# Value product of the dilation-16 attention group: rounded weights and their rests in columns of their own

## The chip, the cores and the metric

The program runs on one core of one Trainium2 chip. The metric is the device time of one execution in microseconds (us); lower is better. A core has a matmul engine (TensorE; PE in the profile, PEld for its weight loads), a vector engine (VectorE, DVE), a scalar engine (ScalarE, ACT), GpSimd (POOL) and SyncE (SP), which issues the transfers. Each engine works through its own queue in order.

## The reference, cut to what matters

The reference is one step of a two-layer decoder trunk. Layer 0 mixes tokens with windowed attention in three head groups, with dilations 1, 4 and 16, over 1024 prompt positions and 16 heads of 64 channels; layer 1 pools. A gated two-matrix channel mixer follows each. What the change touches is the attention of the prompt:

```python
s = jnp.einsum("nbqhd,nbkhd->nbhqk", qb, kb).astype(jnp.float32) * SCALE
s = s + bias[:, np.clip(rel, 0, SPAN)]
s = jnp.where(valid[None, :, None], s, NEG_INF)
m = jnp.max(s, axis=-1)
p = jnp.exp(s - m[..., None])
l = jnp.sum(p, axis=-1)
o = jnp.einsum("nbhqk,nbkhd->nbqhd", p.astype(v.dtype), vb).astype(jnp.float32)
...
o = o / l[..., None]
```

The last product, `p` times `vb`, is the value product. All is float32.

## The kernel before, in words

**Split numbers.** The matmuls run on a rounded float32 type. To keep precision each operand is split into a rounded part ("hi") and its rest ("lo"): ACT copies to the rounded type, and another engine subtracts. A projection is then three matmuls for every pair of operands (L120), with weights split into `w_hi` (ACT, L99) and `w_lo` (POOL, L100).

**Units.** The attention is done in 24 units, a unit being a pair of heads `hp` (0 to 7) and a group `g` (2, then 1, then 0). While the projections of one unit run on PE, the attention of the unit before runs between them. After each projection step (three matmuls at L120) the function `between()` advances a clock by one and emits what is due on a list: for block `i` of 128 queries the scores at 6i+1, the transpose of the weights (`probs_t`) at 6i+15, the value product (`pv`) at 6i+24, and for every second block the finish (`finish_o`) at 6i+26. The splitting of the next unit's queries (`pack_q`, L397 to L399) and keys (`pack_k`, L408 to L410) is emitted at clocks 29 to 46.5 and 50 to 59. So each engine's queue has the order of that list.

**One block.** PE makes scores (L455 where a block has 128 keys, L462 where 256). DVE adds the bias (L456) and reduces (L464), ACT takes the exponential (L467). PE transposes the weights into one PSUM buffer `pt` (L475), ACT rounds them into `phl` (L479), DVE subtracts for the rest (L480). The values were transposed earlier, and stand in `vhl`, rounded part and rest side by side (L443, L444).

**The value product.** For each head, `pv_mm` multiplies the 128 columns of `vhl` (64 rounded, 64 rests) first with the rounded weights, then with their rests, accumulating into the same columns of `u.o` (L489). Each block of group 2 takes four matmuls of 128 columns. Half of the partitions of `u.o` then hold the product with the rounded values, the other half the product with the rests of the values. One tile `u.o` (one PSUM bank, three buffers) serves two blocks and both heads. At the end of the second block ACT copies the half with the rests over to the partitions of the other half (L508), and two clocks later `finish_o` adds both halves and puts the sum in place (DVE, L525).

In this document "step 0" to "step 7" are the eight value products of a unit, and "pair 0" to "pair 3" the four pairs of steps that share a finish.

Of the kernel before, what the change touches and what calls it, by code (L numbers as in the profile page):

```python
# [11 lines left out]
F32 = mybir.dt.float32  # L12
F32R = mybir.dt.float32r
AF = mybir.ActivationFunctionType
# [33 lines left out]
def trunk(ctx: ExitStack, tc: tile.TileContext, a, out):  # L48
    nc = tc.nc
# [31 lines left out]
    raws, split, nxt, more = {}, {}, [0, 0, 0], [None]  # L81
# [200 lines left out]
    with ExitStack() as ph:  # L282
        qp = ph.enter_context(tc.tile_pool(name="qkv", bufs=1))
        mmp = ph.enter_context(tc.tile_pool(name="mmp", bufs=1, space=PSUM))
        app = ph.enter_context(tc.tile_pool(name="app", bufs=1, space=PSUM))
# [150 lines left out]
        def transpose_v(u, half):  # L436
            ps = app.tile([128, 4, 2, 64], F32, name="vt", tag="misc")
            for j in range(4):
                i = 4 * half + j
                nc.tensor.transpose(ps[:, j].rearrange("p a d -> p (a d)"),  # L440
                                    u.raw[2][:, T - 128 * i - 128:T - 128 * i], ident)
            v = qp.tile([128, 4, 2, 128], F32R, name="vhl", tag="vhl", bufs=2)
            nc.scalar.activation(v[:, :, :, 0:64], ps, AF.Copy)  # L443
            nc.vector.tensor_sub(v[:, :, :, 64:128], ps, v[:, :, :, 0:64].bitcast(F32))  # L444
            u.v[half] = v

        def scores(u, i):
            w = 256 if has_prev(u.g, i) else 128
# [34 lines left out]
        def pv_mm(u, j, b0, b1, first):  # L483


            q = (j + b0) % 2
            for h in range(2):
                for x in range(2):
                    nc.tensor.matmul(u.o[:, h, 128 * q:128 * (q + b1 - b0)], u.v[j // 4][:, j % 4, h, :],  # L489
                                     u.pt[j][0][:, h, x, 128 * b0:128 * b1], start=first and h + x == 0, stop=True,  # L490
                                     skip_group_check=True)

        def pv(u, j):
            first = j % 2 == 0
            if first:
                u.o = app.tile([128, 2, 256], F32, name="o", tag="o", bufs=3)
                if j and u.pt[j - 1][1] == 256:
                    pv_mm(u, j - 1, 1, 2, True)
                    first = False
            pv_mm(u, j, 0, 1 if j % 2 else u.pt[j][1] // 128, first)  # L500
            if j % 2:

                x = 256 * (j // 2 % 2)
                tmp = (part[:, 0, x:x + 256] if (u.hp, u.g) != order[23] else
                       qp.tile([128, 256], F32, name="ot", tag="ot", bufs=1))
                u.tmp = tmp, u.o
                for h, (own, other) in enumerate(((A, B), (B, A))):
                    nc.scalar.activation(tmp[own], u.o[other, h], AF.Copy)  # L508

        def finish_o(u, i):  # L510

            if i == 0:
                u.og = ogs[0]()[:, :T]
                ogs.rotate(-1)
            tmp, o = u.tmp
            if u.g == 0:
                dst, split = u.og[:, 256 * i:256 * i + 256], lambda t: t
            elif u.g == 1:
                dst = u.og.rearrange("p (n q r) -> p r n q", n=2, r=4)[:, i]
                split = lambda t: t.rearrange("p (n q) -> p n q", n=2)  # L520
            else:
                dst = u.og.rearrange("p (s r) -> p r s", r=16)[:, 4 * i:4 * i + 4]
                split = lambda t: t.rearrange("p (n q) -> p n q", n=4)
            for h, own in enumerate((A, B)):
                nc.vector.tensor_add(dst[own], split(o[own, h]), split(tmp[own]))  # L525


        stat_d = {}
# [278 lines left out]
        def attend(u, tasks, gap=6):  # L807


            u.v, u.p, u.pt = [None, None], {}, {}  # L810
            if u.g:
                u.st = qp.tile([128, 8, 2, 2], F32, name="st", tag=f"st{u.g}", bufs=2)
            else:
                u.others = qp.tile([128, 3, 8, 2, 2], F32, name="st", tag="st0", bufs=2)
                u.st = u.others[:, 0]
            steps = []
            for i in range(8):
                steps += [(6 * i + 1, lambda i=i: scores(u, i)), (6 * i + 15, lambda i=i: probs_t(u, i)),
                          (6 * i + 24, lambda i=i: pv(u, i))]
                if i % 2:  # L820
                    steps.append((6 * i + 24 + 2, lambda i=i: finish_o(u, i // 2)))
            for half in range(2):
                steps.append((24 * half + 4, lambda half=half: transpose_v(u, half)))

            def others():
                for g in range(2):
                    nc.sync.dma_start(out=u.others[:, 1 + g].rearrange("p b h e -> p b (h e)"),
                                      in_=stat_d[u.hp][g].rearrange("(b p) e -> p b e", p=128))

            if u.g == 0:  # L830
                steps.append((26, others))
            steps.append((47, lambda: store_stats(u)))
            for i in range(tasks):
                steps += [(gap * i + 4, lambda: task(extra)), (gap * i + 7, lambda: task(behind))]
            plan.extend(sorted(steps, key=lambda x: x[0]))
            clock[0] = 0.0
# [64 lines left out]
        for n, (hp, g) in enumerate(order):  # L901
            u = units[hp, g] = Unit()
# [8 lines left out]
            for i, (which, c) in enumerate(seq):  # L911
# [12 lines left out]
                ps = mmp.tile([128, 352], F32, name="mm", tag="mm", bufs=2)  # L924
# [58 lines left out]
        for n, ct in enumerate(OUT):  # L983
# [9 lines left out]
            for c in range(3):  # L993
                c0, c1 = CHUNKS[c]
                ps = mmp.tile([128, 352], F32, name="mm", tag="mm", bufs=2)
# [416 lines left out]
```

## Time and profile before

| | |
|---|---|
| median of 3 runs | 2903.01 us (2902.28 to 2905.36) |
| the profiled execution | 2902.76 us, span 2900.8 us |
| PE busy | 2786.3 us (96%) |
| DVE, ACT, POOL busy | 1629.2 us (56%), 1357.9 us (47%), 1409.8 us (49%) |
| the 24 attention units | about 75 to 1231 us of the span |
| value matmuls (L489) | 864, of which 256 in the 8 units of group 2 |

A view of the profile lists instructions with start (us from the start of the span), duration, engine, line, operation and tiles written and read; `xN` merges N of them. Square brackets hold the time for which the engine was idle before, and what ended the wait. A busy share is an average over the program: what bounds a unit is read from that unit's rows.

### The profile page before, as it was taken

What the parts mean: (1) busy time and instruction counts of PE and PEld (TensorE: products, weight loads), DVE (VectorE), ACT (ScalarE), POOL (GpSimd) and SP (SyncE); (2) the same over time, 40 slices, a digit from 0 to 9 for tenths busy, and PEclk for the clock granted to TensorE, in tenths of its full rate; (3) what the DMA queues carried; (4) which work ended last, traced back from release to release, by engine and by line L of the source; (5) the groups of instructions that cost most, each with busy time, mean ns of one, the idle gap of its engine ahead of it and who ended that gap; (6) DMA issues with size and microseconds to landing.
All of it is one profiled execution on the core that took longest, in us unless ns stands there. A gap on an engine that the chain in (4) does not pass through costs nothing.

```text
span 2900.8 us, 46721 instructions
## 1 busy us (share of the span) xinstructions
PE 2786.3 (96%) x18109; PEld 2741.8 (95%) x18109; DVE 1629.2 (56%) x3196; ACT 1357.9 (47%) x2748; POOL 1409.8 (49%) x999
## 2 busy tenths in 40 slices
PE   6999999999999999999999999988899999999998
PEld 5999999999999999889999999988899999999998
DVE  6666756675666566765323334787756333435555
ACT  5565665566556655534222323445442333334443
POOL 4235443545354435445434434566753443445785
PEclk9999999999999999999999999999999999999999
DMA  3234333433343324438222222333332226223543
GB/s 117 58 85 124 95 86 87 122 90 91 82 128 94 87 86 145 139 95 106 67 73 73 66 73 73 109 103 108 119 103 66 73 67 81 67 72 98 182 139 102
DMA packets 203949, 277.80 MB, mean 96 GB/s; under 512 B 70272, under 2 KB 154096, under 8 KB 203728
## 3 DMA queue, kind: packets, MB, share of 16 engines
q1 hardware_dynamic: 203680, 274.80, 34.3%
q8 instruction: 142, 2.33, 0.3%
q14 instruction: 79, 0.65, 0.1%
q10 hardware_dynamic: 48, 0.02, 0.0%
HBM read 251.89 MB, written 23.34 MB: 95 GB/s over the span
## 4 chain that ended last, share of the span: by engine, by line
PE 77%; DVE 13%; ACT 3%; issue 3%; POOL 2%; DMA 1%; SPq 0%; DVEq 0%; ACTq 0%; POOLq 0%
PE mm L120 68%; PE o L489 2%; DVE k L408 2%; PE s L462 1%; POOL w_lo L100 1%; PE pt L475 1%; DVE conv L1117 1%; DVE conv L1114 1%; DVE x L399 1%; ACT w_hi L99 1%; PE s L455 1%; DVE x L397 1%; DVE sums L1225 1%; DVE sc L634 1%; PE spv L768 1%
## 5 line engine op out<-in xcount | busy, mean ns | idle before, releaser
L120 PE MATMUL mm<-hh,w_hi 128*128 128x352 f32 (+2 forms) x4064 | 1343.9, 331 | 13.9 <-ACT w_hi L99 6.9
L120 PE MATMUL mm<-hh,w_lo 128*128 128x352 f32 (+2 forms) x4064 | 1308.8, 322 | 10.4 <-POOL w_lo L100 10.4
L120 PE MATMUL mm<-hl,w_hi 128*128 128x352 f32 (+2 forms) x4064 | 1308.0, 322 | 2.4 <-DVE hl L255 2.4
L100 POOL TENSOR_TENSOR w_lo<-w_raw,w_hi 128x1024 fp32r<-128x1024 f32 x346 | 848.5, 2456 | 672.1 <-ACT w_hi L99 649.3
L120 PEld LDWEIGHTS mm<-hh,w_hi 128*128 128x128 f32 x4064 | 772.7, 190 | 20.7 <-ACT w_hi L99 7.5
L120 PEld LDWEIGHTS mm<-hh,w_lo 128*128 128x128 f32 x4064 | 771.2, 190 | 13.1 <-POOL w_lo L100 13.1
L120 PEld LDWEIGHTS mm<-hl,w_hi 128*128 128x128 f32 x4064 | 773.2, 190 | 4.7 <-DVE hl L255 3.9
L1114 DVE SCALAR_TENSOR_TENSOR conv<-gate,convp,conv 128x336 f32<-128x336 f32 (+1 forms) x176 | 253.6, 1441 | 428.6 <-ACT conv L1112 412.2
L99 ACT ACTIVATE w_hi<-w_raw 128x1024 fp32r<-128x1024 f32 x348 | 363.4, 1050 | 259.9 <-PE mm L120 240.1
L120 PE MATMUL mm<-gh,w_hi 128*128 128x352 f32 (+2 forms) x1056 | 340.8, 323 | 7.6 <-DVE conv L1104 6.3
L120 PE MATMUL mm<-gh,w_lo 128*128 128x352 f32 (+2 forms) x1056 | 340.1, 322 | 3.5 <-POOL w_lo L100 3.5
L120 PE MATMUL mm<-gl,w_hi 128*128 128x352 f32 (+2 forms) x1056 | 339.8, 322 | 0.6 <-POOL gl L1106 0.6
L1052 DVE TENSOR_TENSOR x<-x,mm 128x352 f32<-128x352 f32 (+2 forms) x312 | 157.1, 511 | 257.1 <-PE mm L120 256.5
L467 ACT ACTIVATE p<-p,st 128x128 f32<-128x128 f32 (+1 forms) x384 | 170.0, 443 | 202.4 <-DVE st L464 201.7
L1106 POOL TENSOR_TENSOR gl<-conv,gh 128x352 fp32r<-128x352 f32 (+2 forms) x132 | 124.5, 944 | 238.1 <-ACT gh L1105 233.4
L120 PEld LDWEIGHTS mm<-gh,w_hi 128*128 128x128 f32 x1056 | 199.6, 189 | 9.3 <-DVE conv L1104 7.6
L120 PEld LDWEIGHTS mm<-gh,w_lo 128*128 128x128 f32 x1056 | 200.1, 189 | 4.4 <-POOL w_lo L100 4.4
L120 PEld LDWEIGHTS mm<-gl,w_hi 128*128 128x128 f32 x1056 | 199.8, 189 | 1.1 <-POOL gl L1106 1.1
L480 DVE TENSOR_TENSOR phl<-pt,phl 128x512 fp32r<-128x512 f32 (+1 forms) x192 | 104.6, 545 | 164.2 <-ACT phl L479 163.1
L368 ACT ACTIVATE raw<-mm 128x336 f32<-128x336 f32 (+1 forms) x216 | 144.5, 670 | 102.5 <-PE mm L120 99.1
L1101 ACT ACTIVATE conv<-conv 128x688 f32<-128x688 f32 (+1 forms) x88 | 55.9, 635 | 275.1 <-DVE conv L1114 137.2
L1097 ACT ACTIVATE gate<-mm 128x352 f32<-128x352 f32 (+2 forms) x132 | 59.8, 454 | 224.1 <-PE mm L120 222.5
(190 smaller groups left out, 3190.3 us busy)
## 6 DMA issues: line engine op xcount, KB each, us to landing
w_raw<-in_w_in SPq DMA_DIRECT2D x176, 512.0 KB
w_raw<-in_w_out SPq DMA_DIRECT2D x88, 512.0 KB
w_raw<-in_w_qkv SPq DMA_DIRECT2D x72, 512.0 KB
x<-qd SPq DMA_DIRECT2D x48, 256.0 KB
kc<-in_cache_k SPq DMA_DIRECT2D x48, 256.0 KB
vc<-in_cache_v SPq DMA_DIRECT2D x48, 256.0 KB
x<-c_d SPq DMA_DIRECT2D x42, 256.0 KB
out_new_k<-raw SPq DMA_DIRECT2D x8, 516.0 KB
```

The lines of the kernel that those rows point to most:

```text
L99: nc.scalar.activation(hi, raw, AF.Copy)
L100: (eng or nc.gpsimd).tensor_sub(lo, raw, hi.bitcast(F32))
L120: nc.tensor.matmul(ps, l, r, start=first and i == 0, stop=last and i == n - 1)
L368: nc.scalar.activation(stream(raw[:, :T], u.g, c0, t1, which > 0), ps[:, :w].rearrange("p (s r) -> p s r", r=DILS[u.g]), AF.Copy, scale=si ...
L408: nc.vector.tensor_copy(keys[h][own, 0, t], raw[own, t])
L467: nc.scalar.activation(p[:, h, :w], p[:, h, :w], AF.Exp, bias=u.st[:, i, h, 0:1], scale=-1.0, accum_out=u.st[:, i, h, 1:2])
L480: nc.vector.tensor_sub(phl[:, :, 1, :w], ps[:, :, :w], phl[:, :, 0, :w].bitcast(F32))
L489: nc.tensor.matmul(u.o[:, h, 128 * q:128 * (q + b1 - b0)], u.v[j // 4][:, j % 4, h, :], u.pt[j][0][:, h, x, 128 * b0:128 * b1], start=firs ...
L1052: nc.vector.tensor_add(xT[ct][:, c0:c1], xT[ct][:, c0:c1], ps)
L1097: nc.scalar.activation(gate[:, 2 + s:2 + e], group(tiles8(w, c), c), AF.Copy)
L1106: nc.gpsimd.tensor_sub(self.gl[f][:, s:e], conv[:, s:e], self.gh[f][:, s:e].bitcast(F32))
L1114: nc.vector.scalar_tensor_tensor(conv[:, :n], gate[:, j:j + n], cw[j], conv[:, :n], op0=ALU.mult, op1=ALU.add)
```

## The change

Only group 2 (the one with dilation 16, where each block reads its own 128 keys) takes another value product. The rounded weights and their rests lie side by side as 256 moving columns, and one matmul per head puts their two products into columns of their own. A pair of blocks therefore has two output tiles `u.o`, one for each head, each with 256 columns of the rounded weights and 256 of the rests. The values of the second head are stored rest first, so that in both heads the wanted partitions hold the product with the rounded values. When the second block is done, ACT copies the product of the value rests with the rounded weights as before, and a new DVE addition adds to it the product of the rounded values with the weight rests. The finish adds the last part. The product of value rests with weight rests is not used any more in group 2. The three buffers of `u.o` stay three.

```diff
-            v = qp.tile([128, 4, 2, 128], F32R, name="vhl", tag="vhl", bufs=2)
-            nc.scalar.activation(v[:, :, :, 0:64], ps, AF.Copy)
-            nc.vector.tensor_sub(v[:, :, :, 64:128], ps, v[:, :, :, 0:64].bitcast(F32))
-            u.v[half] = v
+            v = qp.tile([128, 4, 4, 64], F32R, name="vhl", tag="vhl", bufs=2)
+            hi, lo = v[:, :, 0:4:3], v[:, :, 1:3]
+            nc.scalar.activation(hi, ps, AF.Copy)
+            nc.vector.tensor_sub(lo, ps, hi.bitcast(F32))
+            u.v[half] = v.rearrange("p j x d -> p j (x d)").rearrange("p j (h e) -> p j h e", h=2)
...
         def pv_mm(u, j, b0, b1, first):
+            if u.g == 2:
+                for h in range(2):
+                    nc.tensor.matmul(u.o[h][:, :, 128 * (j % 2):128 * (j % 2) + 128], u.v[j // 4][:, j % 4, h, :],
+                                     u.pt[j][0][:, h, :, 0:128], start=first, stop=True, skip_group_check=True)
+                return
...
         def pv(u, j):
-                u.o = app.tile([128, 2, 256], F32, name="o", tag="o", bufs=3)
+                u.o = [app.tile([128, 2, 256], F32, name="o", tag="o", bufs=3) for _ in range(2 if u.g == 2 else 1)]
+                if u.g < 2:
+                    u.o = u.o[0]
...
                 for h, (own, other) in enumerate(((A, B), (B, A))):
-                    nc.scalar.activation(tmp[own], u.o[other, h], AF.Copy)
+                    nc.scalar.activation(tmp[own], u.o[h][other, 0] if u.g == 2 else u.o[other, h], AF.Copy)
+                    if u.g == 2:
+                        nc.vector.tensor_add(tmp[own], u.o[h][own, 1], tmp[own])
...
         def finish_o(u, i):
-                nc.vector.tensor_add(dst[own], split(o[own, h]), split(tmp[own]))
+                nc.vector.tensor_add(dst[own], split(o[h][own, 0] if u.g == 2 else o[own, h]), split(tmp[own]))
```

## Rows read from the trace of the kernel before

**Rows 1.** The page: PE's busy time, and the chain that ended last.
```profile
PE 2786.3 (96%) x18109; PEld 2741.8 (95%) x18109; DVE 1629.2 (56%) x3196; ACT 1357.9 (47%) x2748; POOL 1409.8 (49%) x999
...
PE 77%; DVE 13%; ACT 3%; issue 3%; POOL 2%; DMA 1%; SPq 0%; DVEq 0%; ACTq 0%; POOLq 0%
```

**Rows 2.** Timeline of PE, head pair 2: a value step of group 2.
```profile
397.39 0.56 PE L489 MATMUL o<-phl,vhl 128*128 128x128 f32 x4
...
398.00 0.32 PE L120 MATMUL mm<-hl,w_hi 128*128 128x352 f32 x1
398.16 0.32 PE L120 MATMUL mm<-hh,w_lo 128*128 128x352 f32 x1
```

**Rows 3.** The same, a score block: two matmuls of 256 columns.
```profile
390.98 0.40 PE L455 MATMUL s<-k,x 128*128 128x256 f32 x2
391.22 0.32 PE L120 MATMUL mm<-hh,w_hi 128*128 128x344 f32 x1
```

**Rows 4.** Groups by line and shape: of that unit alone, then of all units.
```profile
L489 PE MATMUL o<-phl,vhl 128*128 128x128 f32 x32 | 4.5, 261 | 0.0
...
L525 DVE TENSOR_TENSOR x<-o,ot 64x256 f32<-64x256 f32 x8 | 3.3, 416 | 0.1
```

**Rows 5.** Timeline of ACT and DVE, head pair 2, pair 0.
```profile
381.28 0.77 ACT L508 ACTIVATE part<-o 64x256 f32<-64x256 f32 x2 [0.25 <-PE o L489]
...
382.06 0.42 DVE L456 TENSOR_TENSOR p<-s,bias 128x256 f32<-128x256 f32 x1 [0.81 <-PE s L455]
...
387.89 0.42 DVE L480 TENSOR_TENSOR phl<-pt,phl 128x256 fp32r<-128x256 f32 x1
```

**Rows 6.** Timeline of ACT and DVE, head pair 2, from pair 1 on.
```profile
390.80 0.77 ACT L508 ACTIVATE part<-o 64x256 f32<-64x256 f32 x2
...
390.81 0.43 DVE L480 TENSOR_TENSOR phl<-pt,phl 128x256 fp32r<-128x256 f32 x1 [1.38 <-ACT phl L479]
391.42 0.42 DVE L456 TENSOR_TENSOR p<-s,bias 128x256 f32<-128x256 f32 x1 [0.18 <-PE s L455]
...
394.58 0.17 DVE L371 TENSOR_SCALAR ks<-mm 128x8 f32<-128x8 f32 x1 [0.25 <-ACT raw L368]
...
401.11 1.23 DVE L525 TENSOR_TENSOR x<-o,part 64x256 f32<-64x256 f32 x2
```

**Rows 7.** Timeline of PE, head pair 2: steps 1 and 6, and a wait.
```profile
380.69 0.56 PE L489 MATMUL o<-phl,vhl 128*128 128x128 f32 x4
...
388.37 0.44 PE L475 MATMUL pt<-consts,p 128*128 128x128 f32 x2 [0.55 <-DVE phl L480]
...
400.86 0.56 PE L489 MATMUL o<-phl,vhl 128*128 128x128 f32 x4
```

**Rows 8.** Timeline of PE, head pair 3: steps 6 and 7.
```profile
542.20 0.56 PE L489 MATMUL o<-phl,vhl 128*128 128x128 f32 x4
545.46 0.22 PE L489 MATMUL o<-phl,vhl 128*128 128x128 f32 x1
547.60 0.55 PE L489 MATMUL o<-phl,vhl 128*128 128x128 f32 x3 [1.92 <-DVE phl L480]
```

**Rows 9.** Chain that ended last in 517 to 552 us (head pair 3).
```profile
531.16 0.44 DVE p L456
...
534.34 0.17 DVE ks L371
...
545.14 0.50 DVE x L525
...
545.65 0.59 DVE x L525
...
547.12 0.43 DVE phl L480
```

**Rows 10.** Stretches: PE, PEld, DVE, ACT, POOL busy, granted clock, DMA, GB/s.
```profile
500.00:501.70 1.70, 0.51 (x4) 0.51 (x5) 1.56 (x7) 0.72 (x2) 0.00 (x0) 1.00 0.00 0
501.70:505.10 3.40, 3.40 (x14) 3.40 (x13) 2.08 (x9) 1.92 (x4) 0.82 (x1) 0.50 0.30 119
```

## The prediction

> **What bounds the kernel now.** The page comes first: PE is busy for 96% of the span and holds 77% of the chain that ended last, DVE 13% [rows 1]. Read over the whole program, that says that fewer matmuls are time saved. But the change sits in eight stretches of some 30 us, the units of group 2, so their rows were read next, engine by engine. In an even unit (head pair 2) PE runs on with one wait for DVE, 0.55 us before the transpose at 388.37 [rows 7]. In an odd unit (head pair 3) DVE sets the pace at the end: the chain of that stretch enters DVE at 531.16, passes through ACT and the projection evacuations without slack to 534.34 and stays on DVE's queue until the weight rests at 547.12 [rows 9], while PE stands 1.92 us in the middle of step 7 [rows 8]. The reason is the same everywhere: the splitting of the next unit's keys and queries is queued on DVE between the value steps. So a matmul saved on PE is worth its time only where DVE is not late, and every DVE instruction added ahead of that backlog is worth its full time.
>
> **The change part by part.**
>
> *Matmuls.* A unit of group 2 has 32 value matmuls of 128 columns [rows 4], four to a step. In step 5 of head pair 2 they begin at 397.39 and the second projection matmul behind them at 398.00; less the 0.16 of one projection matmul (398.00 to 398.16) the four took 0.45 us [rows 2]. Two matmuls of 256 columns whose moving operand lies in two runs, as the new ones' does, take 0.24 us (390.98 to 391.22) [rows 3]. A step saves 0.21 us; 64 steps would give 13.4 us if PE set the pace throughout.
>
> The new matmul also writes its output in two runs of 128 columns, which no row of before shows. The Trainium skill's page "PSUM — Partial Sum Buffer" (Specifications) speaks against the change here: a non-contiguous pattern slows matmuls markedly. [Rows 3] show only that a moving operand in two runs costs nothing beside the row's own length. By the rule with a doubled matmul the step would cost 0.48 us and the saving be gone (a rival below); I take 0.24, since within a run the columns still lie side by side.
>
> *Values, copies.* The split of `vhl` moves as many elements as before in runs of 64 as before, and ACT's copies keep their shape: nothing.
>
> *Additions.* There are 64 new DVE additions of 64x256, two to a pair of steps. The nearest rows are the finishes: 0.42 us where they write side by side, as these do [rows 4], 0.61 where they scatter (1.23 for two) [rows 6]. I take 0.42, so 0.84 for a pair; 0.61 is the upper bound, and nothing (hidden in idle time) the lower one. They wait in DVE's queue for ACT's copies. Behind them stand bias and reductions of the next scores (for which ACT's exponential waits), the rests of the weights (for which PE waits), the key and query splits and the finish.
>
> Pair 0: ACT could begin its copies at 381.06 rather than 381.28 (it was idle 0.25 before) [rows 5], since the first matmul of step 1, begun at 380.69 [rows 7], ends earlier; first copy done 381.44, additions 381.47 to 382.30. The bias of the next scores began at 382.06, after 0.81 us of idle time that hides the rest [rows 5]: it is late by 0.26. From there DVE's queue had no gap to the rests that end at 388.31 and release PE at 388.37 [rows 5, 7]. So PE passes that wait 0.26 later, less the 0.21 of step 0 that was saved before: 0.05 late. The 0.21 of steps 1 and 2 goes into the wait.
>
> Pair 1: ACT copies 390.80 to 391.57, DVE is free at 391.24 [rows 6], so the additions run from 391.26 to 391.67 and, behind the second copy, to 392.10. The bias waited at 391.42 [rows 6] and begins at 392.12: 0.70 late. In the odd unit the same place is the unbroken chain of [rows 9] through exponential, query split and evacuation to L371, so DVE's backlog (from 394.58 in [rows 6]) begins 0.70 late. Lower bound nothing, if some gap of ACT and DVE takes it up.
>
> Pair 2: another 0.84 within the backlog. Its finish began at 401.11 [rows 6].
>
> *The wait that is added.* Two tiles for a pair out of three buffers: the second tile of a pair must take the buffer of the first tile of the pair before. Its matmul waits until the finish has read that tile; behind it in PE's queue stand the projections. At the first two pairs that just fits. At pair 3 it does not, even as things are: the finish of pair 2 runs from 401.11, and step 6 begins at 400.86 [rows 6, 7]; in the odd unit 545.05 (its first half ends at 545.65, [rows 9]) against 542.20 [rows 8]. Until now the third buffer hid that.
>
> Even unit: the first addition of the finish ends at 401.11 + 0.61 + 0.70 + 0.84 = 403.26; 0.06 to release PE (as 388.31 to 388.37), 0.12 for the matmul: PE goes on at 403.44. Before it went on at 400.86 + 0.45 = 401.31. Late 2.13; less 0.21 in step 7, with the 0.05: +1.97 us.
>
> Odd unit: 545.65 + 0.70 + 0.84 + 0.06 + 0.12 = 547.37 against 542.65: 4.72 late. Step 7 then arrives at 545.46 + 4.72 = 550.18, and finds its weight rests done (547.12 + 0.43 + 1.54 = 549.09): the old wait is swallowed. It ends at 550.42 against 547.60 + 3 x 0.1125 = 547.94. With the 0.05: +2.53 us.
>
> The other units repeat these two patterns (four of each kind): 4 x (1.97 + 2.53) = +18.0 us.
>
> *The clock.* After a pause of PE (busy 0.51 of 1.70 us) the granted clock went to 0.50, the lower of its two levels (1.2 of 2.4 GHz), for 3.40 us [rows 10], which costs about half of that, 1.7. A wait of over 4 us in each odd unit should bring such falls too; one stretch with such a pause is no rule, so I count two more: +3.4. Bounds: none, and one in each of the eight units, 13.6.
>
> *Sum.* 2902.76 (the profiled execution; its span is 2900.80, the median of the runs 2903.01, so nothing is gained by choosing) + 18.0 + 3.4 = **2924.2 us**.
>
> **The rivals.** A difference under 0.2% (5.8 us) is about what a measurement here can't tell from none.
>
> *The additions are hidden, only the buffer wait counts* (0.20). For it: DVE's idle time before the scores [rows 5]. Against: the chain of [rows 9] has no gap. Even unit: 401.11 + 0.61 + 0.18 = 401.90, 0.59 late, less 0.21 twice (steps 0 and 7): +0.17. Odd: 545.83, 3.18 late, step 7 ends at 545.46 + 3.18 + 0.24 = 548.88, +0.94, less 0.21: +0.73. Eight units: +3.6, so 2906.4. Of its 0.20 I count 0.12 under the bound and 0.08 over it.
>
> *PE keeps its gain* (0.10; the other side). If the finish is always done before the next pair's second matmul, PE's queue alone decides: 2902.8 - 13.4 = 2889.4. It needs the first half of the finish of pair 2 to end by about 400.9 and 542.3. For it: PE's share of the chain [rows 1] and the fit at the first two pairs. Against: in [rows 6 to 9] that finish ends 0.8 and 3.4 us later already. A part of this that stays within 0.2% gets 0.02.
>
> *More of the same* (0.12): the additions at 0.61 (0.39 more for a pair, three pairs, eight units: 9.4) or a fall of the clock in every unit (13.6 rather than 3.4: 10.2). 2933.6 or 2934.4.
>
> *Slow two-run outputs* (0.05). At 0.24 us more for a step, 64 steps add at most 15.4 to the forecast: 2939.6. Nothing in the rows shows it. That would be the rule of the Trainium skill's page "PSUM — Partial Sum Buffer".
>
> **How the numbers follow.** The forecast itself has 0.53. Slower: 0.53 + 0.12 + 0.05 + 0.08 = 0.78. Same: 0.12 + 0.02 = 0.14. Faster: 0.08. Range: from the hidden additions, 2906, to the dear ones, 2934; what lies below (the kept gain) and above is just under 2 in 10.
>
> **What would show it.** Value matmuls of group 2: 128 of them, two to a step, 0.24 us. PE waiting for DVE L525 (the finish) at the second matmul of step 6, about 1.8 us in even units and over 4 in odd ones, eight times; the wait at step 7 in odd units gone. A DVE addition at 0.42 us behind each copy, and the biases behind pair 1 0.7 us later against PE. The prediction is wrong if these waits are missing (the buffers turn otherwise than I read them), if DVE's backlog shrinks because its splits, whose times swing with POOL's work, fall elsewhere, or if the waits at step 6 are made good in the following unit.

## The result and the profile after

The changed kernel takes 2924.39 us (median of 6 runs, 2918.75 to 2925.08), the kernel before 2904.31 (6 runs, 2902.28 to 2910.98): ratio 1.006 with a 95% interval of 1.0046 to 1.0074, 20.1 us slower, against a forecast of 2924.2. The profiled execution took 2925.07 us with a span of 2923.3, 22.5 more than before. The total is right; below it turns out that two of its terms were wrong in opposite directions, by 6.7 and by 9.0 us.

The page of the changed kernel answers to [rows 1]:

```profile
PE 2790.3 (95%) x17981; PEld 2744.0 (94%) x17981; DVE 1643.6 (56%) x3260; ACT 1359.0 (46%) x2748; POOL 1410.2 (48%) x999
...
PE 75%; DVE 14%; ACT 5%; issue 3%; POOL 2%; DMA 1%; SPq 0%; DVEq 0%; ACTq 0%; POOLq 0%
```

128 matmuls are gone from PE's count, and PE is busy 4.0 us longer. That is the first sign that PE ran slower somewhere. DVE's 64 additions are there.

What PE waited for in the first 1260 us (total us, times, longest), before:

```profile
PE o L489 <- DVE phl L480: 11.5, 9, 2.3
PE pt L475 <- DVE phl L480: 9.9, 15, 1.4
```

and after:

```profile
PE o L491 <- DVE x L537: 22.7, 8, 4.3
PE pt L477 <- DVE phl L482: 18.6, 18, 2.7
```

The first row of after is the buffer wait: a value matmul that waits for the finish, once in each of the eight units. The eight are not alike: 2.47, 4.31, 1.70, 2.20, 1.71, 4.32, 1.71 and 4.30 us in head pairs 0 to 7. The wait of value matmuls for weight rests, first row of before, is gone but for 2.2 us in the other groups. Waits of the transposes for weight rests have nearly doubled.

In the even unit of [rows 2, 7], PE's timeline after (head pair 2, steps 5 to 7):

```profile
403.56 0.40 PE L491 MATMUL o<-phl,vhl 128*128 128x256 f32 x2
403.79 0.32 PE L120 MATMUL mm<-hh,w_hi 128*128 128x352 f32 x1
...
407.97 0.28 PE L491 MATMUL o<-phl,vhl 128*128 128x256 f32 x1
409.95 0.36 PE L491 MATMUL o<-phl,vhl 128*128 128x256 f32 x1 [1.70 <-DVE x L537]
```

A step takes 0.23 us (403.56 to 403.79). Step 6 begins at 407.97, does its first head, and stands for 1.70 us until the finish of pair 2 has read the buffer.

DVE's timeline in the same unit answers to [rows 5, 6]:

```profile
397.31 0.42 DVE L482 TENSOR_TENSOR phl<-pt,phl 128x256 fp32r<-128x256 f32 x1 [1.39 <-ACT phl L481]
397.72 0.88 DVE L520 TENSOR_TENSOR part<-o,part 64x256 f32<-64x256 f32 x2
398.62 0.42 DVE L458 TENSOR_TENSOR p<-s,bias 128x256 f32<-128x256 f32 x1
...
401.79 0.17 DVE L371 TENSOR_SCALAR ks<-mm 128x8 f32<-128x8 f32 x1 [0.25 <-ACT raw L368]
...
408.32 0.87 DVE L520 TENSOR_TENSOR part<-o,part 64x256 f32<-64x256 f32 x2
409.23 1.21 DVE L537 TENSOR_TENSOR x<-o,part 64x256 f32<-64x256 f32 x2
```

The additions stand where the forecast had them: between weight rests and bias at pair 1, and just ahead of the finish at pair 2. The chain of waits of that stretch shows the release:

```profile
408.32 0.42 DVE part L520
...
408.77 0.44 DVE part L520
...
409.23 0.59 DVE x L537
409.82 0.14 issue
409.95 0.36 PE o L491
```

In an odd unit (head pair 5) the wait is 4.3 us, and something follows it. PE's timeline:

```profile
848.11 0.54 PE L491 MATMUL o<-phl,vhl 128*128 128x256 f32 x1 [4.32 <-DVE x L537]
848.44 0.49 PE L120 MATMUL mm<-hh,w_hi 128*128 128x336 f32 x1
848.73 0.48 PE L120 MATMUL mm<-hl,w_hi 128*128 128x336 f32 x1
...
852.89 0.32 PE L120 MATMUL mm<-hh,w_hi 128*128 128x344 f32 x1
853.05 0.32 PE L120 MATMUL mm<-hl,w_hi 128*128 128x344 f32 x1
```

Behind the wait a projection matmul starts every 0.29 us, some microseconds later every 0.16. The same two stretches as windows (columns as in [rows 10]):

```profile
843.50:848.10 4.60, 0.29 (x3) 0.07 (x2) 4.41 (x8) 0.20 (x1) 3.92 (x4) 1.00 0.84 267
848.10:852.60 4.50, 4.49 (x19) 4.50 (x20) 3.93 (x7) 0.78 (x1) 1.91 (x2) 0.62 0.34 135
```

PE was busy for 0.29 of 4.60 us, and in the next 4.5 us the granted clock is 0.62 on the mean, that is, the lower of the two levels for most of it. (4.50 at 0.62 loses 1.7 us.) The buffer waits of head pairs 0, 1, 3 and 7 are followed by such a stretch too. Those of 2, 4 and 6 (1.70 and 1.71 us) are not; head pair 6 has its slow stretch behind another wait, 1.23 us before the transpose at 984.32.

In head pair 3, the odd unit from which the forecast was worked out, the lateness comes in two waits, the first before the last transpose (PE):

```profile
547.19 0.44 PE L477 MATMUL pt<-consts,p 128*128 128x128 f32 x2 [2.66 <-DVE phl L482]
552.35 0.55 PE L491 MATMUL o<-phl,vhl 128*128 128x256 f32 x1 [2.20 <-DVE x L537]
```

### The profile page after: what moved, and what is told of

The parts are those of the page before. It is cut to its first block, busy times and chain, and to the rows that moved or that the text cites. A ratio compares the mean times of both kernels' runs of the same rounds, so it can differ in the third digit from the quotient of the medians.

```text
span 2923.3 us, 46529 instructions
## 1 busy us (share of the span) xinstructions
PE 2790.3 (95%) x17981; PEld 2744.0 (94%) x17981; DVE 1643.6 (56%) x3260; ACT 1359.0 (46%) x2748; POOL 1410.2 (48%) x999
## 4 chain that ended last, share of the span: by engine, by line
PE 75%; DVE 14%; ACT 5%; issue 3%; POOL 2%; DMA 1%; SPq 0%; DVEq 0%; ACTq 0%; POOLq 0%
PE mm L120 67%; PE o L497 2%; DVE k L408 2%; PE s L464 1%; POOL w_lo L100 1%; DVE conv L1129 1%; PE pt L477 1%; DVE conv L1126 1%; DVE x L399 1%; ACT w_hi L99 1%; PE spv L780 1%; DVE part L520 1%; PE vt L440 1%; DVE phl L482 1%; DVE sums L1237 1%
## 5 line engine op out<-in xcount | busy, mean ns | idle before, releaser
L120 PEld LDWEIGHTS mm<-hh,w_lo 128*128 128x128 f32 x4064 | 775.6, 191 | 13.2 <-POOL w_lo L100 13.2
```

The source lines that it names most:

```text
L120: nc.tensor.matmul(ps, l, r, start=first and i == 0, stop=last and i == n - 1)
```

## Where the 20 us are

The unit stretches of group 2, from one unit's value transposes to the next unit's, were summed over its eight units. Windows of the changed kernel: an even stretch (head pair 2), two odd ones (3 and 5), and the sum of all eight:

```profile
369.30:418.20 48.90, 45.03 (x302) 42.92 (x301) 34.33 (x88) 29.09 (x74) 28.97 (x17) 1.00 0.41 102
511.90:563.20 51.30, 44.95 (x276) 43.84 (x274) 36.25 (x88) 26.85 (x70) 30.18 (x17) 0.90 0.49 136
...
808.30:857.90 49.60, 42.85 (x274) 41.88 (x273) 35.61 (x88) 26.76 (x70) 30.59 (x17) 0.97 0.50 141
...
sum 393.50, PE 354.10 PEld 343.37 DVE 276.65 ACT 221.49 POOL 220.48; mean PE 44.26 PEld 42.92 DVE 34.58 ACT 27.69 POOL 27.56
```

The sum before, then that of the kernel `e3_matmuls` below, which has the new matmuls and no additions or second tile:

```profile
sum 369.90, PE 354.16 PEld 345.51 DVE 254.91 ACT 217.17 POOL 218.40; mean PE 44.27 PEld 43.19 DVE 31.86 ACT 27.15 POOL 27.30
```

```profile
sum 364.50, PE 341.74 PEld 331.91 DVE 256.36 ACT 217.72 POOL 218.52; mean PE 42.72 PEld 41.49 DVE 32.04 ACT 27.22 POOL 27.31
```

`e3_matmuls` has the same PE instructions as the changed kernel, at a granted clock of 1.00 in six of the stretches and 0.99 and 0.96 in two. So:

- the matmuls saved are worth 354.16 - 341.74 = 12.4 us of PE's time;
- the changed kernel needs 354.10 - 341.74 = 12.4 us more for the same instructions: that is the slower clock (0.90 to 0.97 in six of its eight stretches);
- PE's idle time rose from 369.90 - 354.16 = 15.7 to 393.50 - 354.10 = 39.4: 23.7 us of waits.

Together 23.7 + 12.4 - 12.4 = 23.7 (393.5 - 369.9 = 23.6); the rest of the program gave back 1.1 (22.5 - 23.6). This is an account of PE's time in one execution. It does not say what would come back without one of its terms: while PE waits for DVE, a faster PE only waits longer. The same account for the other kernels, from the profiled execution of each (us, summed over the eight stretches; the last column is the difference of the medians to the kernel before on the same chip):

| kernel | stretches | PE busy | PE idle | whole, median |
|---|---|---|---|---|
| before | 369.9 | 354.2 | 15.7 | 0 |
| changed | 393.5 | 354.1 | 39.4 | +20.1 |
| e1_two_tiles | 387.7 | 362.4 | 25.3 | +10.7 |
| e2_adds | 384.1 | 359.8 | 24.3 | +12.9 |
| e3_matmuls | 364.5 | 341.7 | 22.8 | -6.7 |
| e4_no_adds | 381.4 | 350.1 | 31.3 | +7.9 |
| e7_pairs_0_3 | 380.0 | 351.2 | 28.8 | +6.2 |
| e6_before_keys_late | 360.3 | 351.9 | 8.4 | -6.2 |
| e5_keys_late | 355.8 | 342.0 | 13.8 | -16.3 |
| e8_filled_waits | 388.4 | 362.8 | 25.6 | +21.1 |
| e9_queries_late | 353.7 | 342.6 | 11.2 | -17.7 |

A profiled execution lies up to 3.8 us from the median of its kernel. Those of `e1_two_tiles`, `e6_before_keys_late` and `e8_filled_waits` are the longest of their runs, those of `e2_adds`, `e4_no_adds` and `e9_queries_late` the shortest, so in a row the stretches and the last column need not agree to better than that.

## The experiments

**Each part alone.** First the matmuls: one tile as before, and the second block of 128 columns overwrites the first, so that half of the products of group 2 is missing.

```diff
+ nc.tensor.matmul(u.o[:, h].rearrange("p (x q) -> p x q", x=2), u.v[j // 4][:, j % 4, h, :],
+                  u.pt[j][0][:, h, :, 0:128], start=h == 0, ...)
```

> The two matmuls of 256 columns for a step alone: one output tile as before, no new addition. The second block of a pair overwrites the first, so half of the products of group 2 are missing. Theory (what is saved before a wait for DVE goes into that wait): 1.3 us in an even unit, 0.5 in an odd one, 7 us in all: 2896. Rival (PE's queue decides everywhere): 64 x 0.21 = 13.4 us, 2889.5. Rival (two-run outputs slow a matmul): 2903 or more.

Measured: 2899.17 us, ratio 0.9977 (0.9966 to 0.9988), -6.7. Of the 12.4 us saved on PE about half comes out at the end of the program; in the stretches idle time takes back 7.1 (22.8 - 15.7), 4.6 of it in the four odd units. There a matmul saved in front of a late DVE becomes a wait.

Then the buffers: the kernel before with one output tile for each head in group 2, four matmuls of 128 columns as before, and no additions.

```diff
-                u.o = app.tile([128, 2, 256], F32, name="o", tag="o", bufs=3)
+                u.o = [app.tile([128, 2, 256], F32, name="o", tag="o", bufs=3) for _ in range(2 if u.g == 2 else 1)]
```

> The kernel before, with one output tile for each head in group 2 and nothing else changed (four matmuls of 128 columns for a step, no new additions). Theory (the buffer wait counts by itself): PE waits for the finish at step 6 in all eight units, about 0.7 us in even units and 3.2 us in odd ones, where the old wait of step 7 is swallowed; from the rows of before this is 3 x 0.7 + 0.3 + 4 x 1.3 = 7 us, and up to 4 us more for falls of the clock: 2910 to 2914. Rival (PE's queue decides, or another buffer is taken): no such wait, 2903.

Measured: 2916.57 us, ratio 1.0035 (1.0024 to 1.0046), +10.7: as the theory had it (7 to 11 over 2903, if the difference is compared rather than the time). Its waits show where:

```profile
PE o L490 <- DVE x L532: 14.5, 8, 3.1
```

Eight times, up to 3.1 us: the second tile alone makes the wait, without one more DVE instruction.

Then the additions: the kernel before with 64 additions of the same shape and place into a spare tile.

```diff
                     nc.scalar.activation(tmp[own], u.o[other, h], AF.Copy)
+                    if u.g == 2:
+                        nc.vector.tensor_add(spare[own], u.o[own, h], tmp[own])
```

> The kernel before, with 64 additions of 64x256 behind the copies of group 2, of the same shape as the new ones but into a spare tile, so the output is the reference's. Theory (DVE's queue carries them into PE's waits): the transpose of step 4 0.26 later, then 0.7 to 1.5 us at steps 6 and 7: about 1.0 in an even unit and 1.8 in an odd one, 11 us, 2914. Rival (DVE's idle time hides them): 2903 to 2905.

Measured: 2918.81 us, ratio 1.0047 (1.0031 to 1.0062), +12.9. The theory had 11. It is rather an upper bound for what the additions cost the kernel before, because this version has a wait of its own. In it both heads share one tile, and ACT's timeline shows the second copy standing behind the first addition, which reads the same tile:

```profile
539.27 0.38 ACT L510 ACTIVATE part<-o 64x256 f32<-64x256 f32 x1
545.98 0.38 ACT L510 ACTIVATE part<-o 64x256 f32<-64x256 f32 x1 [6.32 <-DVE spare L512]
```

**The changed kernel without the additions** (the products of rounded values with weight rests are left out in group 2):

```diff
-                    if u.g == 2:
-                        nc.vector.tensor_add(tmp[own], u.o[h][own, 1], tmp[own])
```

> The changed kernel without its 64 new additions, so the products of rounded values and weight rests are left out in group 2. Theory: only the buffer wait is left against the saved matmuls, 0.2 us in an even unit and 0.7 in an odd one, 3.6 us, plus one or two falls of the clock: 2906 to 2909, and so 15 to 18 us of the change's cost belong to the additions together with the wait they lengthen. Rival (the buffer wait alone is the cost): as the changed kernel, 2920 or more.

Measured: 2913.76 us, ratio 1.003 (1.0018 to 1.0042), +7.9, against +3.6 with one or two clock falls in the forecast. The account explains the difference: idle time rose by 31.3 - 15.7 = 15.6, less 12.4 saved is +3.2 us, what the arithmetic of waits had given (3.6); the slower clock took another 350.1 - 341.7 = 8.4. So the additions have 20.1 - 7.9 = 12.2 us of the change's cost, less than the 15 to 18 expected. Its buffer wait:

```profile
PE o L491 <- DVE x L535: 15.2, 8, 3.2
```

**The additions at pairs 0 and 3 alone** (in pairs 1 and 2 these products are left out):

```diff
-                    if u.g == 2:
+                    if u.g == 2 and j in (1, 7):
```

> The changed kernel with the new additions only at pairs 0 and 3; in pairs 1 and 2 the products of rounded values and weight rests are left out. Theory (pair 1 delays the chain into DVE's backlog by 0.7, pair 2 adds 0.84 ahead of the finish; pair 0 costs 0.26, pair 3 nothing): close to the kernel without additions, 8.7 + 8 x 0.26 = 10.8 us over the kernel before, 2914. Rival (each pair's additions cost alike): half-way between without and with, 14.5 us over, 2918.

Measured: 2912.07 us, ratio 1.0019 (1.001 to 1.0027), +6.2, no slower than without any addition (+7.9); the 0.26 us that the expectation gave to pair 0 in each unit does not show. So the 32 additions of pairs 1 and 2 cost the whole 20.1 - 6.2 = 13.9 us, and the 32 of pairs 0 and 3 nothing measurable: same instruction, same length.

**The backlog moved away.** If the cause is the finish of pair 2 standing behind the key splits, the changed kernel must gain when these splits are emitted later. `pack_k` moves by eight clocks in the units whose attention is of group 2, so that it falls behind pair 2's finish:

```diff
-[50 + 3 * j for j in range(4)]
+[50 + 8 * (g == 1) + 3 * j for j in range(4)]
```

> The changed kernel with the key splits of the unit that is projected meanwhile emitted eight clocks later (58, 61, 64 and 67 rather than 50 to 59), only beside the attention of group 2. Theory (the finish of pair 2 is late because it and the additions stand behind the key splits on DVE): the finish comes before the splits, the waits at step 6 (1.7 us in even, 4.3 in odd units) and the one before the last transpose mostly go, some of it comes back at the start of the next unit, which finds DVE late: 2906 to 2912. Rival (the third tile's reuse or the additions cost as such, wherever the splits stand): 2920 or more.

> The kernel before with the same later key splits. Theory: in odd units the waits for the weight rests (1.4 before the last transpose, 1.9 in step 7) go, about 8 to 10 us in four units, less what the next unit loses: 2895 to 2901. Rival (DVE's work is only moved, the next unit waits as long): 2903.

Measured: changed kernel with later keys 2889.58 us, ratio 0.9947 (0.9933 to 0.996), -16.3; the kernel before with later keys 2899.59, ratio 0.9977 (0.9969 to 0.9986), -6.2. The second came as expected, the first at least 16 us faster than expected: the loss of 20.1 has become a gain of 16.3. PE's timeline of the changed kernel with later keys (head pair 2, steps 5, 6 and 7) has no wait:

```profile
394.18 0.40 PE L491 MATMUL o<-phl,vhl 128*128 128x256 f32 x2
...
397.41 0.40 PE L491 MATMUL o<-phl,vhl 128*128 128x256 f32 x2
...
400.45 0.40 PE L491 MATMUL o<-phl,vhl 128*128 128x256 f32 x2
```

because on DVE the finish of pair 2 (L537) now runs ahead of the key casts (L408):

```profile
395.81 1.25 DVE L537 TENSOR_TENSOR x<-o,part 64x256 f32<-64x256 f32 x2
...
397.43 0.87 DVE L408 CAST k<-raw 64x512 fp32r<-64x512 f32 x2
```

Between these two kernels the change is worth 2889.58 - 2899.59 = -10.0 us. That PE's busy time in the stretches differs by as much (342.0 - 351.9 = -9.9) does not account for it: the stretches themselves are only 355.8 - 360.3 = -4.5 apart, since idle time is 5.4 higher (the wait of the transposes is 13.2 us against 9.0). The other 5.6 us lie outside the stretches, where the later keys cost the kernel before 8.8 us (2900.0 - 360.3 against 2900.8 - 369.9) and the changed kernel 4.3 (2889.9 - 355.8 against 2923.3 - 393.5). That some of the gain would come back in the next unit was expected; why it differs between the two was not tested.

**The clock by itself.** To keep PE busy in the buffer wait, the changed kernel repeats the first matmul of step 6 (same result) 12 to 26 times, by unit:

```diff
+again = (16, 26, 12, 16, 12, 26, 12, 26)[u.hp] if j == 6 else 0
-for h in range(2):
+for h in [0] * again + [0, 1]:
```

> The changed kernel in which PE fills most of the wait of step 6 by repeating that step's first matmul (12 to 26 times, 1.4 to 3.1 us; each time it starts its columns anew, so the output is the same). Theory (a good part of the loss is the granted clock, which falls after these waits: in the stretches of group 2 PE is busy 29 us at the lower level against 4 before): the falls go, the end of the wait stays, 8 to 11 us less than the changed kernel: 2913 to 2917. Rival (the waits themselves are the whole cost): as the changed kernel, 2922 to 2925.

Measured: 2927.19 us against 2906.09 on the same chip, ratio 1.0072 (1.0059 to 1.0084): no faster than the changed kernel. In group 2 the stretches fell from 393.5 to 388.4, as the theory had it in direction. By the account the repeats took some 17.4 us (146 at 0.12), so the slower clock is down from 12.4 to 362.8 - 341.7 - 17.4 = 3.7, while waits and repeats together are up from 39.4 to 43.0: of 8.7 us of clock, 5.1 came out. The filling was not exact: in head pair 3 a wait of 2.44 us and its slow stretch stayed, in head pair 1 the repeats ran on about 1.3 us past the release. And the stretches of group 0 (seven, one between each two units of group 2) grew. Their sum in the changed kernel, then one of them and the sum in this one:

```profile
sum 371.20, PE 355.56 PEld 343.72 DVE 225.48 ACT 229.79 POOL 146.97; mean PE 50.79 PEld 49.10 DVE 32.21 ACT 32.83 POOL 21.00
```

```profile
1054.90:1107.20 52.30, 49.08 (x331) 48.17 (x330) 31.32 (x82) 30.68 (x74) 19.05 (x12) 0.97 0.33 94
...
sum 378.90, PE 359.50 PEld 347.16 DVE 230.79 ACT 230.68 POOL 149.52; mean PE 51.36 PEld 49.59 DVE 32.97 ACT 32.95 POOL 21.36
```

Here four of the seven show a granted clock of 0.97, in the changed kernel two; half of the growth of 7.7 us is busy time (3.9), half waits. That filled waits shorten the stretches of group 2 is seen in one execution of each kernel (5.1 us). What the slower clock costs the whole program is not shown, and stays open.

**One more move.** In the changed kernel with later keys, PE still waits before the transpose of step 4 (13.2 us in all). There the second query split was moved behind it as well:

```diff
-(29, 29 + 3, 44.5, 44.5 + 2)
+(29, 29 + 3 + 2.5 * (g == 1), 44.5, 44.5 + 2)
```

> The changed kernel with the key splits late as in e5, and the second query split beside group 2 emitted at clock 34.5 rather than 32, behind the rests of step 3. Theory (PE's wait before the transpose of step 4, 1.2 to 1.5 us in eight units, is for rests that stand behind this split on DVE): most of it goes, 6 to 10 us less than e5: 2880 to 2884. Rival (the split delays the next rests instead): 2888 to 2890.

Measured: 2888.41 us against 2906.09, ratio 0.9936 (0.9923 to 0.995), -17.7; the interval overlaps that of the version it starts from. In time the rival was right, though the waits are not the ones that it named:

```profile
PE pt L477 <- DVE phl L482: 7.7, 14, 1.4
...
PE o L491 <- DVE x L537: 3.3, 8, 0.5
```

The wait of the transposes fell to 7.7, as the theory had it, and eight short buffer waits (3.3 us) appeared behind it.

## Why the prediction was right, and where it was not

**Matmuls: right.** 0.23 us for a step where 0.24 was taken, 12.4 us saved in sum where 13.4 was worked out. Writing an output in two runs of 128 columns costs nothing that the rows show. The rule of the Trainium skill's page "PSUM — Partial Sum Buffer" (Specifications), that a non-contiguous pattern slows matmuls, is not borne out for this pattern.

**Additions: right in price and place.** The group by form has 422 ns (0.42 was taken) and ACT's copies in front:

```profile
L520 DVE TENSOR_TENSOR part<-o,part 64x256 f32<-64x256 f32 x64 | 27.0, 422 | 13.5 <-ACT part L518 12.2
```

At pair 1 the bias begins 398.62 - 397.31 = 1.31 us after the weight rests, before 0.61 [rows 6]: the forecast 0.70 later. From L371 to the finish of pair 2 it is 409.23 - 401.79 = 7.44, before 401.11 - 394.58 = 6.53 [rows 6]: 0.91 more, forecast 0.84. Pair 0 costs nothing, as forecast (0.05), and `e7_pairs_0_3` shows it.

**The buffer wait: right in two even units, too dear in the others.** Where the forecast had about 1.8 and over 4 us, PE waits 1.70 or 1.71 in three even units (2.47 in head pair 0) and 4.3 in three odd ones (2.20 in head pair 3). From the windows, idle time added less time saved: an even stretch of head pairs 2 and 4 lost 1.9 us (forecast 1.97), one of head pair 6 1.2. The four odd ones lost 0.6 to 2.0, on the mean 1.5, where 2.53 was forecast, and head pair 0 lost 0.2, where it was counted as an even unit like the others. The sum is 23.7 - 12.4 = 11.3 rather than 18.0. The step that failed is "the other units repeat these two patterns", with DVE's splits taken at their lengths of before. The prediction had named their swing as what might go wrong. In every odd unit a split ahead of the finish came out shorter: in head pair 5 the second query cast (DVE timeline, before and after)

```profile
824.55 1.91 DVE L397 CAST x<-raw 64x512 fp32r<-64x512 f32 x1
```

```profile
837.52 0.82 DVE L397 CAST x<-raw 64x512 fp32r<-64x512 f32 x1
```

and likewise from 1.36 to 0.47 in head pair 1 and from 1.47 to 0.42 in 7. In head pair 3 the subtractions L399 and L410 went from 2.77 to 1.66 each, but a key cast between them grew (before and after):

```profile
539.41 0.74 DVE L408 CAST k<-raw 64x512 fp32r<-64x512 f32 x1
```

```profile
544.98 1.82 DVE L408 CAST k<-raw 64x512 fp32r<-64x512 f32 x1
```

Over all splits of an odd unit from that query cast on to the finish of pair 2 the backlog is 0.9, 1.1, 1.1 and 1.1 us shorter, 4.2 in sum, against the 4 x (2.53 - 1.5) = 4.1 that are missing; unit by unit the two do not agree (head pair 3 misses 2.0). What these lengths go with shows in the two traces, before and after, where POOL's times are rough: a cast of 64x512 during which POOL did nothing took 0.40 to 0.43 us (81 of them) and a subtraction 0.69 (99), and every longer one (190 and 62) overlaps work of POOL, though some that overlap it stayed short. No experiment varied POOL's work alone. In head pair 0 the additions of pair 1 delayed nothing, the lower bound that the prediction had named: the finish of pair 1 begins 26.2 us into the stretch before and 26.3 after. The rest of its difference stays open.

**The clock: mechanism right, size wrong.** The price of a fall is about as forecast (1.7 us behind the wait of head pair 5; an odd stretch at 0.97 has 42.85 us of busy time where `e3_matmuls` has 41.3 at 1.00). But the forecast counted two more falls, 3.4 us; the stretches show 12.4, in six of the eight units. The bound of the prediction, a fall in every unit, 13.6, is nearly what came. Two were counted because one stretch with such a pause was no rule. The trace of before had more of them: behind the wait of 1.88 us in head pair 1 (255.04) and one of 2.18 at 1081.62, though not behind those of 1.92 and 1.86 in head pairs 3 and 5.

```profile
255.00:260.00 5.00, 4.96 (x22) 4.96 (x23) 4.36 (x8) 1.18 (x3) 0.88 (x1) 0.66 0.04 13
...
1082.00:1085.40 3.40, 3.40 (x14) 3.40 (x13) 1.94 (x7) 1.88 (x3) 0.55 (x1) 0.50 0.24 95
```

With these, and four waits of over 4 us in its own forecast, there was reason to count at least those four.

So 21.4 was forecast as 18.0 + 3.4, and came as 11.3 + 12.4 with 1.1 given back elsewhere. The total is right partly by luck: 6.7 too much for the waits stand against 9.0 too little for the clock.

**The rivals.** Hidden additions: refuted by `e7_pairs_0_3` against the changed kernel, 13.9 us for pairs 1 and 2; by the account 10.6 of it are waits (39.4 - 28.8) and 2.9 clock (354.1 - 351.2). PE keeps its gain: its own condition, a finish done before the next pair's second matmul, was met in `e5_keys_late`, and there it came true in part: 10.0 of the 13.4 us that it named, but only 4.5 of them in the units of group 2. More of the same: of its two halves the dearer additions did not come (422 ns), the clock in nearly every unit did, and the total stayed below its 2934.4 because the waits were shorter. Slow two-run outputs: not seen, 0.23 us for a step.

## What to carry to other kernels

When a tile is split in two and the number of buffers stays, ask which reader the second tile now waits for, and what stands ahead of that reader on its engine: here key splits that could wait were queued ahead of a finish that could not, and moving them turned +20 us into -16. Price an added instruction by its place, not by its length: 32 additions cost nothing where the engine was idle, and the same 32 in a backlog cost 14 us. Where a pause of TensorE is forecast, give the slower clock behind it a term of its own: here it followed all five buffer waits of 2.2 us and more, and none of the three of 1.7.

## What was unexpected of the hardware

- Behind the five buffer waits of 2.20 to 4.32 us PE ran on at the lower clock, behind the three of 1.70 and 1.71 it did not; a wait of 1.23 us before a transpose was followed by it in head pair 6, waits of 1.21 and 1.22 at the same place in head pairs 2 and 4 were not. In PE's busy time the clock took as much (12.4 us) as the net waits (11.3).
- The same DVE cast of 64x512 (L397) took 0.40 to 1.91 us, and the same subtraction (L399) 0.69 to 2.77, in one program; they shift by up to 1.1 us when work around them moves, and none of the long ones ran without POOL at work beside it.
- A read by ACT and a read by DVE of the same PSUM tile did not run side by side in `e2_adds`: ACT stood 6.32 us before its second copy, until DVE's first addition was done. The trace names DVE's addition as what released it; whether the hardware or the order laid down in the program makes this was not tested. In the changed kernel, with a tile for each head, the two copies run back to back (397.31, 0.78 us).
